# A hybrid decoder layer with a 16384-expert PEER block: order of the gathers in the second half's embedding, layout of the gate products, stored low parts, and which engines pad the value weights

## The chip, the cores and the metric

The kernel runs on one core of a Trainium2 chip. The core has TensorE (PE, matrix products, with its weight loads shown as PEld), VectorE (DVE), ScalarE (ACT), GpSimd (POOL) and SyncE (SP); SP and POOL issue all transfers here. The metric is the device time of one execution in microseconds. The result is compared as the median of several runs.

## The reference

One layer on 1024 tokens of width 1024, all in fp32. What matters here is what follows the mixer:

```python
mix = hybrid_mixer(x, ...)                       # z = x @ w_in, RG-LRU branch, GLA branch, m @ w_out
x   = layer_norm(DN_ALPHA * x + mix, ln1_g, ln1_b)
ple = sigmoid(x @ ple_gate_w) * (p @ ple_proj_w)
ffn = peer(x, ...)
x   = layer_norm(DN_ALPHA * x + ffn + ple, ln2_g, ln2_b)

def peer(x, w_q, sub_keys, u_tab, v_tab):
    q = (xt @ w_q).reshape(T, 8, 2, 64)
    s = einsum("thpc,hpkc->thpk", q, sub_keys)   # 8 heads, 2 halves, 128 keys
    top_s, top_i = top_k(s, 16)                  # per half
    ...                                          # 256 candidates -> best 16 per head
    gate = softmax(best_s)
    hid  = gelu(einsum("td,ted->te", xb, u_tab[expert_idx]))
    out  = einsum("te,ted->td", gate * hid, v_tab[expert_idx])
```

So each token picks 128 of 16384 experts. Each expert has a row of 1024 numbers in `peer_u` and one in `peer_v`.

## The kernel before

The 1024 tokens are eight tiles of 128, four to a half. The program does mixer, `post`, mixer, `post` for the two halves, and then `dense`.

**Two ways to compute PEER.** Four tiles (`GT` = 0, 1, 6, 7) gather. `gather_u` fetches, for each of 128 selections, one row of `peer_u` per token by an indirect transfer from POOL (a tile `ug` of 128 x 1024, 0.524 MB), and DVE multiplies it with x1 and sums (L849). `gather_v` fetches rows of `peer_v` by token (`vg`) and PE accumulates them in the PSUM tile `ffn` (L883): four rows make one step of 8 matmuls in the code. Their stationary operand `w32` is a zeroed tile into which a column of the weights is copied on a diagonal (L866, L869); eight such tiles serve a tile of tokens. `ug` and `vg` share one ring of 7 buffers, and of 11 in the dense stage. The other four tiles (`DT` = 4, 5, 2, 3) are computed densely against all experts: `dense_gates` builds for each token a 128 x 128 table of gate values as a matmul of one-hot operands into the PSUM tile `pg`, ACT copies it to `gst` (L990), and it goes to DRAM as `g_d`; `dense` then runs `hidden` and `value` over all 16384 experts.

**fp32 by three products.** Wide matmuls are made of three passes over operands split in a high and a low part (`split`, L259 and L260: ACT rounds, DVE subtracts). `weights` keeps the low part of a weight tile in DRAM in the first half and loads it in the second, so that DVE need not subtract again. The first 60 tiles in the order of the code are kept: the mixer's 56 and four of `w_out`. Not kept are four of `w_out`, eight of `peer_wq` (name `pq`), eight of `ple_gate_w` and four narrower ones of `ple_proj_w`.

**The order of the work.** The scheduler places instructions by priority on each engine; engines run their queues in order. The gathers are a generator beside the main program. `pump(t)` adds `t` times a rate (0.8, 0.6, 1.0, 1.2 in phases 0 to 3) to a credit and advances the generator while credit is left; each row costs 1.46, a routing step 0.7 to 2. `weave` goes round the three parts `us`, `routes`, `vs`, one step each. Phase 2 is the second half's `post` and runs with rate 1.0 at a priority 500 places later; phase 3 is `dense`, 10000 places earlier. Routing of a tile takes 16 selections of scores, the candidates, and the lookup of the keys, nearly all on DVE; tiles 0, 1, 4 and 5 are routed in line, tiles 2, 3, 6 and 7 by `routes`.

**The second half's `post`.** It multiplies by `w_out` (with two of the 32 gate steps after each quarter), normalises, scores the eight heads (a gate step after each), routes tiles 4 and 5, and then does the embedding: four quarters, each with four gate steps, a product with `ple_gate_w` (`plg`) and one with `ple_proj_w` (`plp`). `flow["scored"]` becomes 2 after the routing of tiles 4 and 5.

Of the kernel before, what the change touches and what calls it, by code (L numbers as in the profile page):

```python
# [8 lines left out]
F32 = mybir.dt.float32  # L9
# [4 lines left out]
AF = mybir.ActivationFunctionType  # L14
# [4 lines left out]
P = 128  # L19
# [5 lines left out]
NH = T // HT  # L25
TT = HT // P
# [4 lines left out]
KEYS = 128  # L31
# [22 lines left out]
KG = 4  # L54
RING = 6

LOW = 60

TG = 8

# [7 lines left out]
def kernel(ctx: ExitStack, tc: tile.TileContext, a: dict, out: bass.AP, tap=None):  # L68
    nc = tc.nc
# [8 lines left out]
    dram = ctx.enter_context(tc.tile_pool(name="dram", bufs=1, space=bass.MemoryType.DRAM))  # L78
# [141 lines left out]
    flow = {"it": None, "credit": 0.0, "rate": 0.0, "scored": 0, "phase": 0, "routing": False}  # L220
# [46 lines left out]
    def weights(src, name, shape):  # L267

        raw = early.pop(src.offset, None) if name == "zx" else None
        if raw is None:  # L270
            raw = wpool.tile(shape, F32, name=f"raw_{name}", tag="wraw")
            nc.sync.dma_start(raw, src)
        h = wpool.tile(shape, F32R, name=f"wh_{name}", tag="wh")
        l = wpool.tile(shape, F32R, name=f"wl_{name}", tag="wl")
        key = (src.tensor.name, src.offset)
        if low.get(key) is not None:
            nc.sync.dma_start(l.bitcast(F32), low[key])
            nc.scalar.activation(h, raw, AF.Copy)
        else:
            split(h, l, raw)  # L280
            if key not in low:
                n = len(low)
                low[key] = None
                if n < LOW:
                    low[key] = dram.tile(shape, F32, name=f"low{n}")
                    nc.sync.dma_start(low[key], l.bitcast(F32))
        return h, l

    low = {}
# [567 lines left out]
    def gather_v(ti, idx, idxT, gate, H):  # L857
        ffn = ps_f.tile([P, D], F32, name="ffn")
        nc.tensor.transpose(ffn[:, :P], H[0], ident)
        pw = small.tile([P, P], F32, name="pw")  # L860
        nc.scalar.activation(pw, ffn[:, :P], AF.Copy)
        N = 4
        for ph in range(32 // N):

            w32 = peer.tile([P, 4, N, 32], F32, name="w32", bufs=2)
            nc.vector.memset(w32, 0.0)  # L866
            for c in range(4):
                dst = w32[:, c].rearrange("p r e -> p (r e)")[:, ph * N:ph * N + (N - 1) * 33 + 1:33]
                nc.vector.tensor_copy(dst, pw[:, 32 * c + ph * N:32 * c + ph * N + N])  # L869
            for r in range(N):  # L870

                rows_v = []
                for c in range(4):
                    t = 32 * c + ph * N + r
                    vg = row("vg")
                    nc.gpsimd.indirect_dma_start(out=vg, out_offset=None, in_=a["peer_v"],  # L876
                                                 in_offset=bass.IndirectOffsetOnAxis(ap=idxT[:, t:t + 1], axis=0))
                    rows_v.append(vg)
                    if c < 3:
                        yield 1.46  # L880
                with ExitStack() as side:
                    for n, (e, c) in enumerate((e, c) for e in range(2) for c in (3, 0, 1, 2)):
                        mm = nc.tensor.matmul(ffn[32 * c:32 * c + 32, e * 512:(e + 1) * 512], w32[:, c, r],  # L883
                                              rows_v[c][:, e * 512:(e + 1) * 512], start=ph == 0 and r == 0,
                                              stop=ph == 32 // N - 1 and r == N - 1, skip_group_check=True)
                        if n == 0:

                            side.enter_context(tc.issue_after(mm.ins))
                            side.enter_context(tc.high_priority())
                yield 1.46  # L890
        ln2 = norm2()
        bt = row("bt")
        st = small.tile([P, 2, 6], F32, name="st2")
        nc.sync.dma_start(bt, base_d[ti])
        for e in range(2):
            es = slice(e * 512, (e + 1) * 512)
            nc.vector.scalar_tensor_tensor(bt[:, es], bt[:, es], 0.5, ffn[:, es], op0=ALU.mult, op1=ALU.add)
            nc.vector.bn_stats(st[:, e], bt[:, es])
        finish(ti, bt, st, ln2)

    def weave(*its):

        its = list(its)
        while its:
            stuck = True
            for it in list(its):
                x = next(it, None)
                if x is None:
                    its.remove(it)
                elif x >= 0:  # L910
                    yield x
                if x is None or x >= 0:
                    stuck = False
            if stuck:
                yield -1.0

    def gathers():

        H = {t: [] for t in GT}
        done = []  # L920

        def routes():
            while at[0] < ROUTE:
                yield -1.0
            for t in sorted((t for t in range(T // P) if t % TT >= DIRECT[t // TT]), key=lambda t: (t // TT, t in GT)):

                while t in GT and GT.index(t) > 2 and len(done) < GT.index(t) - 2:
                    yield -1.0
                while flow["scored"] <= t // TT:
                    yield -1.0  # L930
                flow["routing"] = True
                yield from route(t, t in DT, R)
                flow["routing"] = False

        at = [0]

        def us():
            for t in GT:
                while t not in R:
                    yield -1.0  # L940
                for x in gather_u(t, *R[t], H[t]):
                    at[0] += 1
                    yield x

        def vs():
            for t in GT:
                while not H[t]:
                    yield -1.0
                yield from gather_v(t, *R[t], H[t])
                done.append(t)  # L950

        yield from weave(us(), routes(), vs())

    def norm2():
# [7 lines left out]
    def dense_gates(n, g_b, gps, iota):  # L962
# [9 lines left out]
        for tb in range(P // 16):  # L972
            gs = g_b.tile([P, KEYS, 16], F32, name="gst", tag="g")
            for q in range(16 // TG):
# [5 lines left out]
                oj = g_b.tile(B3, F32, name="oj", bufs=2)  # L980
                nc.vector.tensor_tensor(oj, iota, Tb[:, 1, tt, None].to_broadcast(B3), op=ALU.is_equal)  # L981
                for r4 in range(TG // 4):
                    o = gps.tile([P, 4, KEYS], F32, name="pg", tag="g")
                    for r in range(4):
                        t = 4 * r4 + r
                        oi = g_b.tile([P, KEYS], F32, name="oi", bufs=6)
                        nc.scalar.activation(oi, one[:, t], AF.Copy, scale=T3[:, 2, t0 + t:t0 + t + 1])  # L987
                        nc.tensor.matmul(o[:, r], oj[:, t], oi, start=True, stop=True)  # L988
                    q4 = q * TG + 4 * r4
                    nc.scalar.activation(gs[:, :, q4:q4 + 4].rearrange("p i t -> p t i"), o, AF.Copy)  # L990
                    pump(0.9)
            nc.sync.dma_start(g_d[:, :, n * P // 16 + tb].rearrange("g j i t -> j g (i t)"),
                              gs.rearrange("p (g i) t -> p g (i t)", i=8))
# [194 lines left out]
```

## Time and profile before

| | |
|---|---|
| median of 3 runs | 3303.26 us (3296.75 to 3304.23) |
| the profiled execution | 3298.0 us, its span 3296.2 us |
| busy in the span | PE 3042.8, DVE 2375.3, ACT 1228.2, POOL 1160.8 us |
| HBM read, written | 854.76 MB, 81.79 MB |

The span runs from the first to the last instruction. Times within it are counted from its start. The second half's `post` begins near 1118 us, the gates end at 1613.6 us, and the dense stage follows, its first matmuls overlapping the last gates.

### The profile page before, as it was taken

How to read it: one execution, taken by the hardware profiler on the slowest of the kernel's cores; microseconds unless marked ns; L12 is line 12 of the kernel's file. 1: busy time of each engine (PE TensorE's matmuls, PEld its weight loads, DVE VectorE, ACT ScalarE, POOL GpSimd, SP SyncE). 2: the span in 40 equal slices, each digit the busy share in tenths (PEclk: the TensorE clock that was granted, in tenths of full speed). 3: DMA queues.
4: the chain of work that ended last, by engine and by line, in shares of the span. 5: the costliest groups of instructions: out<-in, count | busy, mean ns of one | idle time of the engine just before them, and what ended most of it. 6: DMA issues, size and time to landing. Idle time of an engine off the chain costs nothing.

```text
span 3296.2 us, 48127 instructions
## 1 busy us (share of the span) xinstructions
PE 3042.8 (92%) x17160; PEld 2320.6 (70%) x17160; DVE 2375.3 (72%) x5791; ACT 1228.2 (37%) x2130; POOL 1160.8 (35%) x1034
## 2 busy tenths in 40 slices
PE   8999989797999888658799999999999999999996
PEld 6788777676777676548577777777777777777663
DVE  7556557977888898978887866666666667666333
ACT  6433323263244464648623322222232232223221
POOL 0000000534421445540155444444434545443453
PEclk9999989898999998879899999999999999999997
DMA  5444444777776898976799899999899999988997
GB/s 174 143 172 148 135 160 142 277 293 284 295 263 244 326 312 302 349 252 216 246 376 352 321 338 327 340 338 344 314 340 326 355 335 326 338 328 327 346 322 277
DMA packets 364304, 939.74 MB, mean 285 GB/s; under 512 B 33920, under 2 KB 115968, under 8 KB 359968
## 3 DMA queue, kind: packets, MB, share of 16 engines
q0 software_dynamic: 147456, 536.94, 44.8%
q1 hardware_dynamic: 216608, 399.74, 34.8%
q8 instruction: 134, 2.20, 0.3%
q14 instruction: 106, 0.87, 0.1%
HBM read 854.76 MB, written 81.79 MB: 284 GB/s over the span
## 4 chain that ended last, share of the span: by engine, by line
PE 70%; DVE 14%; DMA 7%; ACT 4%; issue 3%; POOL 1%; SPq 0%; POOLq 0%; DVEq 0%; ACTq 0%
PE ph L263 7%; PE ph L265 7%; PE pv L265 7%; PE pv L263 7%; PE pv L264 7%; PE ph L264 7%; PE ffn L883 7%; DVE ug L849 3%; DMA ug<-in_peer_u_dram,idx 3%; DMA vg<-in_peer_v_dram,idxT 1%; DVE one L979 1%; DVE oj L981 1%; PE pgr L263 1%; PE pgr L264 1%; PE pgr L265 1%
## 5 line engine op out<-in xcount | busy, mean ns | idle before, releaser
L847 POOL DMA_INDIRECT ug<-in_peer_u_dram,idx x512 | 601.3, 1174 | 1345.1 <-DVE bs L776 612.3
L876 POOL DMA_INDIRECT vg<-in_peer_v_dram,idxT x512 | 558.2, 1090 | 756.7 <-DVE ug L849 324.3
L849 DVE SCALAR_TENSOR_TENSOR ug<-ug,x1g 128x1024 f32<-128x1024 f32 x512 | 619.8, 1219 | 47.0 <-DMA ug<-in_peer_u_dram,idx 42.9
L263 PE MATMUL ph<-x1hl,uh 128*128 128x512 f32 x1024 | 408.6, 399 | 0.9 <-DVE sc L737 0.9
L265 PE MATMUL ph<-x1hl,ul 128*128 128x512 f32 x1024 | 407.9, 398 | 0.0
L264 PE MATMUL ph<-x1hl,uh 128*128 128x512 f32 x1024 | 406.6, 397 | 0.0
L264 PE MATMUL pv<-vl,wdh 128*128 128x512 f32 x1024 | 400.5, 393 | 0.0
L263 PE MATMUL pv<-vh,wdh 128*128 128x512 f32 x1024 | 384.3, 393 | 15.9 <-ACT wdh L259 15.9
L265 PE MATMUL pv<-vh,wdl 128*128 128x512 f32 x1024 | 398.7, 393 | 0.0
L259 ACT ACTIVATE uh<-ur 128x512 fp32r<-128x512 f32 x256 | 160.2, 628 | 498.0 <-PE ph L264 489.2
L883 PE MATMUL ffn<-vg,w 128*32 128x512 f32 x2048 | 274.1, 628 | 51.1 <-DMA vg<-in_peer_v_dram,idxT 50.2
L259 ACT ACTIVATE vh<-vr 128x512 fp32r<-128x512 f32 x256 | 160.7, 629 | 356.9 <-PE pv L265 348.7
L260 DVE TENSOR_TENSOR ul<-ur,uh 128x512 fp32r<-128x512 f32 x256 | 175.7, 687 | 159.6 <-ACT uh L259 158.1
L260 DVE TENSOR_TENSOR vl<-vr,vh 128x512 fp32r<-128x512 f32 x256 | 176.3, 690 | 115.2 <-ACT vh L259 115.0
L1062 DVE SCALAR_TENSOR_TENSOR acc<-acc,pv 128x512 f32<-128x512 f32 x256 | 165.0, 681 | 108.8 <-PE pv L265 108.8
L263 PEld LDWEIGHTS pv<-vh,wdh 128*128 128x128 f32 x1024 | 192.8, 188 | 69.3 <-ACT wdh L259 16.1
L263 PEld LDWEIGHTS ph<-x1hl,uh 128*128 128x128 f32 x1024 | 192.4, 188 | 68.6 <-issue 22.6
L265 PEld LDWEIGHTS ph<-x1hl,ul 128*128 128x128 f32 x1024 | 192.4, 188 | 62.1 <-issue 16.8
L265 PEld LDWEIGHTS pv<-vh,wdl 128*128 128x128 f32 x1024 | 192.6, 188 | 58.7 <-issue 16.8
L264 PEld LDWEIGHTS ph<-x1hl,uh 128*128 128x128 f32 x1024 | 192.4, 188 | 55.7 <-issue 11.7
L264 PEld LDWEIGHTS pv<-vl,wdh 128*128 128x128 f32 x1024 | 192.9, 188 | 53.9 <-issue 10.1
L988 PE MATMUL pg<-oi,oj 128*128 128x128 f32 x1024 | 163.2, 301 | 35.9 <-ACT oi L987 25.4
(475 smaller groups left out, 6030.9 us busy)
## 6 DMA issues: line engine op xcount, KB each, us to landing
ur<-in_uT_dram SPq DMA_DIRECT2D x256, 256.0 KB, 6.3
vr<-in_peer_v_dram SPq DMA_DIRECT2D x256, 256.0 KB, 6.3
g_d<-gst SPq DMA_DIRECT2D x32, 1024.0 KB, 8.6
gt<-g_d SPq DMA_DIRECT2D x32, 1024.0 KB, 8.4
raw_zx<-in_w_z_dram SPq DMA_DIRECT2D x16, 512.0 KB, 4.9
raw_zv<-in_w_v_dram SPq DMA_DIRECT2D x16, 512.0 KB, 5.0
raw_zy<-in_w_z_dram SPq DMA_DIRECT2D x16, 512.0 KB, 6.4
raw_ga<-in_w_z_dram SPq DMA_DIRECT2D x16, 512.0 KB, 5.4
```

Of the source, the lines that this page charges most:

```text
L259: nc.scalar.activation(h, src, AF.Copy)
L260: nc.vector.tensor_tensor(l, src, h, op=ALU.subtract)
L263: nc.tensor.matmul(o, wh, xh, start=first, stop=False)
L264: nc.tensor.matmul(o, wh, xl, start=False, stop=False)
L265: nc.tensor.matmul(o, wl, xh, start=False, stop=last)
L847: nc.gpsimd.indirect_dma_start(out=ug, out_offset=None, in_=a["peer_u"], in_offset=bass.IndirectOffsetOnAxis(ap=idx[:, s:s + 1], axis=0))
L849: nc.vector.scalar_tensor_tensor(ug, ug, 1.0, x1, op0=ALU.mult, op1=ALU.mult, accum_out=hid[:, s:s + 1])
L876: nc.gpsimd.indirect_dma_start(out=vg, out_offset=None, in_=a["peer_v"], in_offset=bass.IndirectOffsetOnAxis(ap=idxT[:, t:t + 1], axis=0))
L883: mm = nc.tensor.matmul(ffn[32 * c:32 * c + 32, e * 512:(e + 1) * 512], w32[:, c, r], rows_v[c][:, e * 512:(e + 1) * 512], start=ph == 0 a ...
L979: nc.vector.tensor_tensor(one, iota, Tb[:, 0, tt, None].to_broadcast(B3), op=ALU.is_equal)
L988: nc.tensor.matmul(o[:, r], oj[:, t], oi, start=True, stop=True)
L1062: nc.vector.scalar_tensor_tensor(acc[c][:, es], acc[c][:, es], 0.5 if g == 0 else 1.0, o[c], op0=ALU.mult, op1=ALU.add)
```

## The change

It has four parts.

1. `embedding()` is true from the end of scoring in the second half to the end of phase 2. Then `weave` takes its parts in reverse order and stops after the first that advances, so that value rows come before routing and routing before u rows; `routes` also waits while it is true.
2. The matmul into `pg` writes key by key with the token innermost (a step of 16 bytes), and the copy to `gst` then reads PSUM in order and writes runs of four tokens.
3. Every low part except that of `peer_wq` is kept in DRAM: 16 more tiles.
4. The zeroing of `w32` goes from DVE to POOL, and the copy onto the diagonal from DVE to ACT.

```diff
--- before.py
+++ after.py
@@ -54,7 +54,7 @@
 KG = 4
 RING = 6
 
-LOW = 60
+OWN = ("pq",)
 
 TG = 8
 
@@ -278,12 +278,9 @@
             nc.scalar.activation(h, raw, AF.Copy)
         else:
             split(h, l, raw)
-            if key not in low:
-                n = len(low)
-                low[key] = None
-                if n < LOW:
-                    low[key] = dram.tile(shape, F32, name=f"low{n}")
-                    nc.sync.dma_start(low[key], l.bitcast(F32))
+            if name not in OWN and key not in low:
+                low[key] = dram.tile(shape, F32, name=f"low{len(low)}")
+                nc.sync.dma_start(low[key], l.bitcast(F32))
         return h, l
 
     low = {}
@@ -863,10 +860,10 @@
         for ph in range(32 // N):
 
             w32 = peer.tile([P, 4, N, 32], F32, name="w32", bufs=2)
-            nc.vector.memset(w32, 0.0)
+            nc.gpsimd.memset(w32, 0.0)
             for c in range(4):
                 dst = w32[:, c].rearrange("p r e -> p (r e)")[:, ph * N:ph * N + (N - 1) * 33 + 1:33]
-                nc.vector.tensor_copy(dst, pw[:, 32 * c + ph * N:32 * c + ph * N + N])
+                nc.scalar.activation(dst, pw[:, 32 * c + ph * N:32 * c + ph * N + N], AF.Copy)
             for r in range(N):
 
                 rows_v = []
@@ -898,12 +895,16 @@
             nc.vector.bn_stats(st[:, e], bt[:, es])
         finish(ti, bt, st, ln2)
 
+    def embedding():
+        return flow["phase"] == 2 and flow["scored"] == NH
+
     def weave(*its):
 
         its = list(its)
         while its:
             stuck = True
-            for it in list(its):
+            last = embedding()
+            for it in reversed(its) if last else list(its):
                 x = next(it, None)
                 if x is None:
                     its.remove(it)
@@ -911,6 +912,8 @@
                     yield x
                 if x is None or x >= 0:
                     stuck = False
+                    if last:
+                        break
             if stuck:
                 yield -1.0
 
@@ -926,7 +929,7 @@
 
                 while t in GT and GT.index(t) > 2 and len(done) < GT.index(t) - 2:
                     yield -1.0
-                while flow["scored"] <= t // TT:
+                while flow["scored"] <= t // TT or embedding():
                     yield -1.0
                 flow["routing"] = True
                 yield from route(t, t in DT, R)
@@ -980,14 +983,14 @@
                 oj = g_b.tile(B3, F32, name="oj", bufs=2)
                 nc.vector.tensor_tensor(oj, iota, Tb[:, 1, tt, None].to_broadcast(B3), op=ALU.is_equal)
                 for r4 in range(TG // 4):
-                    o = gps.tile([P, 4, KEYS], F32, name="pg", tag="g")
+                    o = gps.tile([P, KEYS, 4], F32, name="pg", tag="g")
                     for r in range(4):
                         t = 4 * r4 + r
                         oi = g_b.tile([P, KEYS], F32, name="oi", bufs=6)
                         nc.scalar.activation(oi, one[:, t], AF.Copy, scale=T3[:, 2, t0 + t:t0 + t + 1])
-                        nc.tensor.matmul(o[:, r], oj[:, t], oi, start=True, stop=True)
+                        nc.tensor.matmul(o[:, :, r], oj[:, t], oi, start=True, stop=True)
                     q4 = q * TG + 4 * r4
-                    nc.scalar.activation(gs[:, :, q4:q4 + 4].rearrange("p i t -> p t i"), o, AF.Copy)
+                    nc.scalar.activation(gs[:, :, q4:q4 + 4], o, AF.Copy)
                     pump(0.9)
             nc.sync.dma_start(g_d[:, :, n * P // 16 + tb].rearrange("g j i t -> j g (i t)"),
                               gs.rearrange("p (g i) t -> p g (i t)", i=8))
```

## Rows read from the trace of the kernel before

**Rows 1.** The page's first part, busy time by engine (share of the span, instructions)
```profile
PE 3042.8 (92%) x17160; PEld 2320.6 (70%) x17160; DVE 2375.3 (72%) x5791; ACT 1228.2 (37%) x2130; POOL 1160.8 (35%) x1034
```

**Rows 2.** Windows: length, PE, PEld, DVE, ACT, POOL busy; clock, DMA share, GB/s
```profile
545.00:635.00 90.00, 66.22 (x452) 62.23 (x451) 81.81 (x335) 19.69 (x34) 25.96 (x22) 0.84 0.57 201
...
1118.00:1380.00 262.00, 222.35 (x1541) 179.24 (x1534) 248.12 (x674) 173.90 (x389) 136.22 (x102) 0.92 0.95 326
1380.00:1620.00 240.00, 166.93 (x1086) 142.37 (x1085) 206.58 (x610) 156.66 (x369) 58.26 (x48) 0.84 0.75 240
...
1400.00:1460.00 60.00, 33.88 (x207) 23.19 (x211) 51.75 (x144) 21.66 (x54) 32.65 (x26) 0.73 0.74 252
1460.00:1550.00 90.00, 77.71 (x584) 74.32 (x577) 71.23 (x138) 74.44 (x181) 7.46 (x6) 0.92 0.66 203
1550.00:1620.00 70.00, 50.17 (x277) 42.93 (x276) 65.15 (x230) 58.18 (x132) 8.81 (x8) 0.90 0.81 248
1620.00:1830.00 210.00, 201.79 (x940) 146.79 (x941) 170.17 (x472) 59.59 (x100) 101.00 (x88) 0.97 0.92 344
1830.00:2430.00 600.00, 600.00 (x2804) 440.61 (x2803) 416.19 (x769) 173.81 (x293) 273.08 (x259) 1.00 0.91 334
```

**Rows 3.** Windows of value rows alone: PE, PEld, POOL busy, then clock, DMA
```profile
1460.00:1550.00 90.00, 1.54 (x16) 0.26 (x8) 3.83 (x3) 0.92 0.66 203
1550.00:1620.00 70.00, 0.00 (x0) 0.00 (x0) 4.95 (x5) 0.90 0.81 248
1620.00:1830.00 210.00, 24.96 (x192) 5.33 (x192) 47.62 (x44) 0.97 0.92 344
```

**Rows 4.** Chain that ended last, in order of time: start, duration, what
```profile
1656.75 1.85 PE ffn L883 x16
```

**Rows 5.** Waits, 1460 to 1550 and 1400 to 1460: total, times, longest
```profile
POOL vg L876 <- DVE ug L849: 80.6, 1, 80.6
...
PE ffn L883 <- DMA vg<-in_peer_v_dram,idxT: 25.0, 4, 12.2
```

**Rows 6.** Windows of u rows alone: DVE (two records a row), POOL busy, clock, DMA
```profile
1620.00:1830.00 210.00, 50.09 (x82) 53.38 (x44) 0.97 0.92 344
1830.00:2430.00 600.00, 157.59 (x257) 136.46 (x129) 1.00 0.91 334
```

**Rows 7.** Windows, DVE on one tile's score selections, then on its candidates
```profile
1620.00:1740.00 120.00, 20.76 (x128) 0.94 0.95 356
...
1550.00:1620.00 70.00, 7.65 (x65) 0.90 0.81 248
```

**Rows 8.** Groups by line: busy, mean ns of one, idle before and its releasers
```profile
L990 ACT ACTIVATE gst<-pg 128x512 f32<-128x512 f32 x128 | 133.3, 1054 | 14.0 <-DMA g_d<-gst 9.6 <-PE pg L988 4.2
L683 ACT ACTIVATE sc_st<-psc 128x512 f32<-128x512 f32 x32 | 17.5, 595 | 4.5 <-DVE list L739 4.2 <-PE psc L681 0.3
L988 PE MATMUL pg<-oi,oj 128*128 128x128 f32 x1024 | 163.2, 301 | 35.9 <-ACT oi L987 25.4 <-DVE oj L981 8.9 <-ACT gst L990 1.6
L263 PE MATMUL pv<-vh,wdh 128*128 128x512 f32 x1024 | 384.3, 393 | 15.9 <-ACT wdh L259 15.9
L260 DVE TENSOR_TENSOR wl_plg<-raw_plg,wh_plg 128x1024 fp32r<-128x1024 f32 x16 | 19.4, 1215 | 3.7 <-ACT wh_plg L259 3.6
L866 DVE MEMSET w<- 128x512 f32 x32 | 15.5, 485 | 26.1 <-PE ffn L883 25.2
L869 DVE COPY w<-pw 128x4 f32<-128x4 f32 x128 | 12.3, 194 | 0.3
L605 ACT ACTIVATE rs<-mv,eps_l 128x1 f32<-128x1 f32 x16 | 4.5, 292 | 58.1 <-DVE mv L603 43.2 <-DVE y L608 6.8 <-DVE acc L608 4.4
L214 POOL MEMSET qk<- 128x256 f32 x1 | 0.3, 302 | 0.0
```

## The prediction

> **What bounds the kernel now.** I read the totals first, then busy time by stage, then the rows' own instructions in those stages, the waits, and the groups by line. TensorE (PE) is busy for 3042.8 us [rows 1] of a span of 3296.2; the 253 us it lacks are all there is to win without removing matmuls. By stage [rows 2]: in the dense stage, 1830 to 2430, PE has no idle time at all, so there every matmul taken out shortens the kernel. Before it, PE idles for 39.7 us in 1118 to 1380 and for 73.1 in 1380 to 1620, while VectorE (DVE) is busy for 248 of 262 and for 207 of 240 us. So the second half's scoring and embedding are set by DVE and, once the gates run (1460 to 1620), by ScalarE (ACT) with 132.6 of 160; the dense stage is set by PE.
>
> Between the two lies a misfit. A step of four value rows gives `ffn` 16 recorded matmuls and takes PE 1.85 us [rows 3, 4]. From 1460 to 1620 one such step runs, and from 1620 to 1830, with PE full, twelve. The reason is in the waits: GpSimd's queue (POOL) stands for 80.6 us in one piece on a value gather whose buffer a u row holds, until DVE gets to that u row's product [rows 5].
>
> **Value rows first.** I walked the credits of `pump` through the code. Both kernels reach the second half's embedding with 52 or 53 u rows of tile 1 and as many value rows of tile 0 written. The embedding pumps 16 x 2.64 + 16 x 0.66 + 64 x 0.9 = 110 credits. Before, they bought rounds of a u row (1.46), a value row (1.46) and a routing step (about 1.1): 28 of each. After, they buy 75 value rows at 1.46, exactly the rest of tile 0, one u row and no routing. The trace agrees with the walk: 80 value rows at the embedding's end by the one, about 82 at 1620 by the other (46 left in the twelve steps that follow).
>
> So twelve steps leave the full stage: 12 x 1.85 = 22 us less PE work there [rows 3, 4]. They land where PE idles 58 us (1400 to 1620: 26.1 + 12.3 + 19.8) [rows 2]. Transfers allow it: that stretch moves 50.8 MB; 19 more rows of 0.524 MB and 5.2 MB of low parts make 66 MB, 300 GB/s, against 344 reached in 1620 to 1830. Term: -22.
>
> What leaves DVE in the embedding: 28 u rows at 1.22 us (50.09 us for 41 rows [rows 6]) = 34, tile 6's selects = 21 [rows 7], and 8 + 4 subtractions for low parts, 1.215 us each and half that for the narrower four [rows 8] = 12. DVE falls from 188 to 121 of 220 us. Tile 0's finish (its second norm, three loads and a store on SP's queue) follows its last value row into the embedding, into the room that DVE gains there.
>
> **Gates.** The eviction into `gst` writes single elements 64 bytes apart and takes 1054 ns; the score's eviction has the same size, reads PSUM too and writes runs, and takes 595 [rows 8]. The new one writes runs of four. Bounds: no gain, or 0.459 us x 128 = 59; I take nearly all, since the length of the runs is what differs; no row has runs of four. 29 us of that lie in the embedding, 29 before 1380.
>
> How much shorter does the embedding get? With the twelve steps PE needs 161.8 + 22 = 184 of the 220 us, so at most 36 us go, and none if other waits take the place. PE stood 25.0 us in four waits for value rows between 1400 and 1460 [rows 5], and these stay. I take a little under half of the 36. Term: -16 (0 to -36).
>
> From 1118 to 1380 ACT's 29 us lie under DVE, which is 95% busy. DVE loses 4 subtractions for `w_out` (4.9) and three or four blocks of `w32` at 0.485 + 4 x 0.194 = 1.26 us [rows 8], about 9 in all. Term: -6 (0 to -9).
>
> **What comes back.** The 28 u rows and 28 routing steps go to the start of the dense stage: 34 + 21 + about 8 for the candidates [rows 7], less 4 for three blocks of `w32`: 59 us more for DVE, which had 170 of 210 us there. Routing's four loads on SP's queue go with it, now among the u and v tiles' loads; a late one delays only routing, which tile 6's u rows need last. That makes 229: 19 us too many, pushed past 1830 where DVE has 184 of 600 us free. Against that the value rows of tile 1 can't start before u of tile 1 ends, so PE has only dense matmuls to do. The dense matmuls' own need of DVE is (416.2 - 157.6) / 600 = 0.43 us for each us of PE [rows 2, 6]. If the surplus comes wholly out of the splits, PE loses 19 / 0.43 = 44 us; if it is only late, nothing. I take a quarter. Term: +10 (0 to +44).
>
> **Low parts.** 16 more tiles are stored in the first half (four of `w_out`, eight of the gate, four narrower ones of the projection), 7.3 MB. Most of it falls into the first embedding, at 201 GB/s with PE idle 23.8 of 90 us [rows 2]. 5.2 MB more make 259 GB/s, under the 344 seen, so transfers hide it; SP's queue holds the loads behind each store until the subtraction is done. If that cover fails, 5.2 MB at 344 GB/s cost 15 us. Term: +3.
>
> **Padding.** 32 memsets leave DVE (485 ns each), and so do the 26.1 us for which DVE stood in front of them, nearly all for PE to give up `w32` [rows 8]. On POOL one costs between 0.30 us (half the size [rows 8]) and 0.60, against gathers of over 1 us; behind it wait gathers, and behind these DVE and PE. The 128 copies cost ACT between DVE's 0.194 and the 0.292 us of a one-element ACTIVATE [rows 8]: 25 to 37 us over the kernel, hidden in the dense stage where ACT is 29% busy [rows 2]. New is that a copy on ACT waits for POOL, and behind it stand ACT's splits, for which PE waits. Bounds 0 and 26 us; since POOL passes a free `w32` well ahead of the rows, I take +2.
>
> **Matmuls into every fourth word.** `pg` is now written with a step of 16 bytes. No row has such an output. The nearest row is again the eviction, which took 1054 / 595 = 1.77 times as long for single elements 64 bytes apart. Bounds: nothing, or 0.77 x 163 us, the group's time on PE, = 126 [rows 8]. I take nothing: PE takes 163.2 / 1024 = 0.159 us for 128 columns here and 384.3 / 1024 = 0.375 for 512 in the dense stage, so it gives PSUM its words more slowly here than PSUM is seen to take them. The Trainium skill (PSUM — Partial Sum Buffer, section "Specifications (TRN2)") speaks against that: it says that any non-contiguous access pattern slows matmuls significantly, and by it the second rival's 3346 would be the forecast.
>
> **Sum.** -22 - 16 - 6 + 10 + 3 + 2 = -29. The profiled execution took 3298.0 us, 1.8 over its span, and lies 5 under the median of 3303.3; set against the median this gives 3274.
>
> **Rivals.**
> *The dense stage starves.* Phase 3 puts gathers and routing 10000 places ahead of the splits, so DVE does them first. If DVE can be filled only to 90%, 189 of the 229 us fit, and 40 / 0.43 = 93 us of PE are lost in place of 10: -22 - 16 - 6 + 93 + 5 = +54, 3357. It decides from 19 us of splits not made up, as 44 us then meet the gain. For it: 81% busy there already. Against: PE was full at that 81%, and the surplus can be done late, with 184 us free behind it.
> *Strided PSUM.* At 1.77 times, PE has 63 us more in each half of the gate steps. The stretch 1400 to 1620 then needs 184 + 63 = 247 of 220 us, and 1118 to 1380 needs 222 + 63 = 285 of 262: -22 + 27 + 23 + 15 = +43, 3346. It decides once PE, not ACT, sets a gate step. For it speaks the eviction's row; against it that no matmul's row does. The rule quoted above would bring it about, and no run so far shows that.
> *Hidden anyway.* PE's queue stands for each late value row. Waits as in 1400 to 1460, some 6 us for a step, at six of the twelve moved steps take back 36 of the 38 us, and nothing measurable is left: 3303, give or take 9. For it: the 25.0 us. Against: then PE had little else to do.
> *All of it.* PE full through the embedding and no price after: -22 - 36 - 9 = -67, 3236. For it: three engines are relieved at once there.
>
> **Chances.** The forecast 0.46 (own range 3258 to 3293), starving 0.16, strided PSUM 0.08, hidden 0.15, all 0.15. A measurement of this kernel tells about 0.3%, 10 us. Faster: the forecast and "all", less a little at the edge, 0.60; same 0.16; slower 0.24. The range leaves out the worse half of the strided and starving cases and the better half of "all": 3236 to 3340.
>
> **What would show it.** Right: about 30 steps of `ffn` before the dense stage in place of 20; no 80 us wait of POOL on a u row there; `gst` near 600 ns; no u rows and no selects between 1460 and the dense stage; DVE over 90% in its first 200 us with PE still full. Wrong: PE idle time after the dense stage's start, matmuls into `pg` longer than 275 ns each, or waits of PE for value rows beyond 25 us.

## The result and the profile after

The changed kernel took 3332.48 us, the median of 4 runs (3327.47 to 3338.22); the kernel before took 3300.01 beside it (3295.29 to 3304.23). The ratio is 1.0106, with a 95% interval of 1.0090 to 1.0122: slower by about 1.1%, where 3274 and a gain were forecast. The profiled execution took 3327.47 us with a span of 3325.7.

The page of the changed kernel: busy time of PE, then PE's and DMA's busy tenths in 40 slices.

```profile
PE 3055.2 (92%) x17160; PEld 2323.9 (70%) x17160; DVE 2338.9 (70%) x5615; ACT 1198.5 (36%) x2258; POOL 1180.7 (36%) x1066
...
PE   8999988797999888888889999999999999999984
...
DMA  5444455877777999899995769999998999999898
```

PE is busy only 12 us longer than before [rows 1], and yet the span is 29.5 us longer. DMA has a hole in slices 22 to 24 (some 1745 to 1995 us), early in the dense stage, and PE's last slice is at 4. The same stages as in [rows 2], and PE's end (length, PE, PEld, DVE, ACT, POOL busy, clock, DMA share, GB/s):

```profile
1118.00:1380.00 262.00, 226.89 (x1568) 183.87 (x1566) 245.11 (x739) 157.85 (x407) 121.04 (x94) 0.93 0.94 325
1380.00:1620.00 240.00, 196.95 (x1333) 150.57 (x1334) 137.78 (x260) 139.57 (x385) 84.79 (x76) 0.91 0.95 328
1400.00:1460.00 60.00, 48.86 (x367) 39.54 (x366) 46.01 (x102) 42.90 (x125) 24.65 (x21) 0.91 0.87 292
1460.00:1550.00 90.00, 77.56 (x612) 64.98 (x610) 47.69 (x56) 65.99 (x192) 28.90 (x25) 0.94 1.02 338
1550.00:1620.00 70.00, 61.19 (x302) 41.59 (x302) 24.86 (x38) 27.96 (x62) 21.93 (x21) 0.92 0.94 342
1620.00:1830.00 210.00, 184.74 (x748) 146.76 (x747) 208.31 (x536) 63.19 (x104) 94.30 (x71) 0.93 0.79 290
...
3215.00:3307.00 92.00, 50.41 (x272) 9.06 (x260) 2.03 (x4) 2.76 (x13) 55.76 (x61) 0.69 0.98 372
```

And the value rows' matmuls alone, answering [rows 3] (PE, PEld, clock, DMA):

```profile
1400.00:1460.00 60.00, 10.05 (x64) 1.85 (x64) 0.91 0.87 292
1460.00:1550.00 90.00, 12.76 (x96) 2.59 (x96) 0.94 1.02 338
1550.00:1620.00 70.00, 11.15 (x80) 2.27 (x80) 0.92 0.94 342
1620.00:1830.00 210.00, 0.00 (x0) 0.00 (x0) 0.93 0.79 290
1830.00:1950.00 120.00, 0.00 (x0) 0.00 (x0) 1.00 0.60 213
3215.00:3307.00 92.00, 50.41 (x272) 9.06 (x260) 0.69 0.98 372
```

Up to 1620 the steps moved as planned: 15 `ffn` steps (240 records at 16 a step) in 1400 to 1620, 31 in all ahead of the first `pv` matmul where there were 20, PE busy 187.6 us in that stretch (184 forecast), DVE's load gone. At the dense start DVE is busy for 208.31 of 210 us, PE has 25.3 us of idle time in place of 8.2, and no value row is used from 1620 to 1950. At the end 17 `ffn` steps (272 records) run alone; before, there were three.

The gates' two edits, first the `pg` matmuls of the kernel before, then those of the changed one with their eviction (ns min/median/max, first and last start):

```profile
L988 PE MATMUL pg<-oi,oj x1024: 270/275/583, 1126.2 to 1612.1; 128*128 128x128 f32 x171
```

```profile
L991 PE MATMUL pg<-oi,oj x1024: 270/275/582, 1132.6 to 1565.6; 128*128 128x128 f32 x171
L993 ACT ACTIVATE gst<-pg x128: 572/584/612, 1134.0 to 1565.9; 128x512 f32<-128x512 f32 x128
```

The eviction fell from 1054 ns [rows 8] to 584, and the gates end 46.5 us earlier. The matmul into every fourth word takes what it took. On that point the measurement decides against the Trainium skill (PSUM — Partial Sum Buffer, section "Specifications (TRN2)"): a median of 275 ns either way, no slowdown for this non-contiguous write.

**Where the time went.** The gathers form a chain: u rows of a tile, its `hid`, its value rows beside the next tile's u rows, and so on through tiles 0, 1, 6 and 7. Its middle, in the kernel before (one tile's rows in 1760 to 2000, last two numbers the first and last start; `ffn<-ident,hid` is the transposition with which tile 1's value rows begin):

```profile
L859 PE MATMUL ffn<-ident,hid x1: 270/270/270, 1841.4 to 1841.4; 128*128 128x128 f32 x1
```

```profile
L832 PE MATMUL pidx<-ident,idf x1: 271/271/271, 1834.2 to 1834.2; 128*128 128x128 f32 x1
```

That `pidx` is tile 6's; tile 7's comes only at 2429.9 (2200 to 2600):

```profile
L832 PE MATMUL pidx<-ident,idf x1: 270/270/270, 2429.9 to 2429.9; 128*128 128x128 f32 x1
```

In the changed kernel both come ahead of tile 1's value rows; the last fence has the two longest waits of 1700 to 1960:

```profile
L850 ACT ACTIVATE hid<-hid x1: 312/312/312, 1772.6 to 1772.6; 128x128 f32<-128x128 f32 x1
...
L856 PE MATMUL ffn<-ident,hid x1: 271/271/271, 1946.0 to 1946.0; 128*128 128x128 f32 x1
```

```profile
L829 PE MATMUL pidx<-ident,idf x2: 271/272/272, 1835.3 to 1940.5; 128*128 128x128 f32 x2
```

```profile
POOL vg L873 <- PE ffn L880: 74.5, 1, 74.5
POOL ug L844 <- DVE idx L827: 71.9, 1, 71.9
```

POOL stands twice, and DMA's share falls with it. From 1759 to 1831 it stands for the indices of tile 6, whose routing the change has put into the dense start: tile 1's u rows are all fetched, and tile 6's can't be. From 1879 to 1954 it stands for an `ffn` step. Tile 1's `hid` was ready at 1772.6, 44 us earlier than before (1816.3), and was transposed only at 1946.0, 105 us later than before. `pidx` and `ffn` share one PSUM buffer. Before, tile 1's `ffn` took it ahead of tile 7's `pidx`; now tile 7's comes first, and DVE finishes that tile's routing only at 1940. Tile 7's routing isn't late, it is some 490 us early: `routes` holds it until tile 0's value rows are done, and these now end in the embedding.

From the start of tile 1's value rows to the last `ffn` matmul's start the chain takes 1435 us before (1841.4 to 3276.1), and 1360 now (1946.0 to 3305.6): 75 of the 105 us were made up, and the 30 that remain are the loss. The dense matmuls end 43 us earlier (last `pv` at 3214.1 in place of 3257.0) and gain nothing.

The transfers show the same loss. From 1950 to the last `ffn` matmul, before and then after (columns as in [rows 2]):

```profile
1950.00:3276.10 1326.10, 1315.56 (x6284) 940.09 (x6280) 817.20 (x1494) 363.86 (x609) 618.68 (x583) 0.99 0.92 334
```

```profile
1950.00:3305.60 1355.60, 1314.40 (x6260) 923.34 (x6259) 807.32 (x1398) 362.32 (x682) 667.34 (x640) 0.98 0.92 338
```

From 1620 to 1950 the changed kernel moves 26 MB less (262 GB/s in place of 341), and behind 1950 it moves 15 MB more (458 in place of 443), with DMA at 0.92 either way. Whether the order of the gathers or this share sets the pace behind 1950 is open.

The tail of the changed kernel (start, duration, and in brackets the idle time before it and its releaser):

```profile
3271.93 1.92 PE L880 MATMUL ffn<-vg,w 128*32 128x512 f32 x16 [1.79 <-DMA vg<-in_peer_v_dram,idxT]
3278.31 3.64 PE L880 MATMUL ffn<-vg,w 128*32 128x512 f32 x16 [4.46 <-DMA vg<-in_peer_v_dram,idxT]
...
3296.32 3.64 PE L880 MATMUL ffn<-vg,w 128*32 128x512 f32 x16 [6.98 <-DMA vg<-in_peer_v_dram,idxT]
3302.97 3.64 PE L880 MATMUL ffn<-vg,w 128*32 128x512 f32 x16 [3.01 <-DMA vg<-in_peer_v_dram,idxT]
```

PE waits for rows at nearly every step. The granted clock of this stretch is 0.69 on average; within single steps it is 1.00 or 0.50. A step takes 1.92 us at the upper level (2.4 GHz), near the 1.85 of the full stage [rows 4], and 3.64 at the lower (1.2 GHz).

### The profile page after: what moved, and what is told of

It reads as the page before. It is cut to its first block, busy times and chain, and to the rows that moved or that the text cites. A ratio compares the mean times of both kernels' runs of the same rounds, so it can differ in the third digit from the quotient of the medians.

```text
span 3325.7 us, 48251 instructions
## 1 busy us (share of the span) xinstructions
PE 3055.2 (92%) x17160; PEld 2323.9 (70%) x17160; DVE 2338.9 (70%) x5615; ACT 1198.5 (36%) x2258; POOL 1180.7 (36%) x1066
## 4 chain that ended last, share of the span: by engine, by line
PE 70%; DVE 13%; DMA 8%; issue 4%; ACT 4%; POOL 1%; SPq 0%; POOLq 0%; DVEq 0%; ACTq 0%
PE ffn L880 7%; PE ph L265 7%; PE ph L263 7%; PE ph L264 7%; PE pv L263 7%; PE pv L264 7%; PE pv L265 7%; DVE ug L846 5%; DMA vg<-in_peer_v_dram,idxT 3%; PE pg L991 2%; DMA g_d<-gst 2%; DMA ug<-in_peer_u_dram,idx 1%; PE pgr L263 1%; PE pgr L264 1%; PE pgr L265 1%
## 5 line engine op out<-in xcount | busy, mean ns | idle before, releaser
L880 PE MATMUL ffn<-vg,w 128*32 128x512 f32 x2048 | 286.1, 657 | 53.3 <-DMA vg<-in_peer_v_dram,idxT 53.2
L880 PEld LDWEIGHTS ffn<-vg,w 128*32 128x32 f32 x2048 | 58.2, 115 | 203.2 <-issue 137.7
```

## The experiments

They ran in groups, each group on one chip; the kernel before, run beside each, had medians from 3295.8 to 3319.4 us. So a ratio is taken against the kernel before on the same chip, and kernels are set against each other only within a group (those with the same number in brackets in the table). How far ratios of different groups can stand apart is seen on one kernel that ran in two: 0.9932 (0.9909 to 0.9954) and 0.9992 (0.9980 to 1.0004). Groups 3 and 5 bear the same chip number, so the chip alone doesn't explain it. The order on each engine is written by a planner, so each edit shifts instructions beyond its own; a few us of any difference can be that.

The table is read from the traces: start of tile 1's value rows; last `pv` and last `ffn` matmul (starts); PE and DVE busy in 1620 to 1830 (210 us).

| kernel | us (before beside it) | ratio | value rows 1 | last pv | last ffn | PE | DVE |
|---|---|---|---|---|---|---|---|
| before | | 1 | 1841.4 | 3257.0 | 3276.1 | 201.8 | 170.2 |
| after | 3332.5 (3300.0) | 1.0106 | 1946.0 | 3214.1 | 3305.6 | 184.7 | 208.3 |
| E1 (1) other parts alone | 3284.6 (3307.6) | 0.9929 | 1836.7 | 3237.6 | 3263.6 | 210.0 | 170.7 |
| E2 (1) value rows first alone | 3318.6 (3307.6) | 1.0034 | 1912.0 | 3268.6 | 3300.6 | 179.5 | 195.6 |
| E3 (1) u rows alone held | 3289.1 (3307.6) | 0.9941 | 1868.3 | 3264.5 | 3271.0 | 193.0 | 196.9 |
| E4 (1) tile 7's routing late | 3311.8 (3307.6) | 1.0011 | 1863.3 | 3263.2 | 3294.1 | 181.6 | 196.5 |
| E5 (2) both | 3278.5 (3295.8) | 0.9953 | 1800.8 | 3259.3 | 3249.3 | 192.1 | 201.4 |
| E9 (3) after, fewer matmuls | 3298.7 (3319.4) | | 2000.5 | 3031.2 | 3276.8 | 170.2 | 196.4 |
| E10 (3) before, fewer matmuls | 3225.6 (3319.4) | | 1848.7 | 3078.9 | 3203.5 | 180.2 | 181.0 |
| E11 (3) after, short products | 3312.6 (3319.4) | 0.9976 | 1911.5 | 3237.5 | 3291.9 | 191.3 | 171.1 |
| E12 (3) layout and padding | 3297.0 (3319.4) | 0.9932 | 1838.1 | 3253.0 | 3273.3 | 206.8 | 169.5 |
| E14 (4) as E5 | 3287.9 (3310.9) | 0.9936 | 1809.0 | 3267.7 | 3257.7 | 191.1 | 199.9 |
| E15 (4) E5, low parts as before | 3279.3 (3310.9) | 0.9911 | 1800.7 | 3260.4 | 3250.0 | 192.4 | 202.5 |
| E16 (4) E5, held to row 64 | 3276.9 (3310.9) | 0.9908 | 1798.6 | 3245.3 | 3247.0 | 209.3 | 185.7 |
| E17 (4) as E1 | 3286.6 (3310.9) | 0.9936 | 1837.6 | 3238.5 | 3264.4 | 210.0 | 170.8 |
| E18 (5) E16, low parts as before | 3271.0 (3296.4) | 0.9921 | 1811.4 | 3244.3 | 3249.3 | 209.7 | 187.8 |
| E19 (5) as E12 | 3293.5 (3296.4) | 0.9992 | 1833.5 | 3248.2 | 3269.2 | 208.5 | 168.8 |

### Which part costs, and through what: E1 to E4

E1 takes the reordering out of the changed kernel; E2 puts it alone (the hunks of `embedding`, `weave` and `routes`) into the kernel before.

```diff
     def embedding():
-        return flow["phase"] == 2 and flow["scored"] == NH
+        return False
```

> The changed kernel with the turn-taking of gathers as before (the other three parts of the change stay). Theory A: the end is set by the chain of gathers (u rows of tile 1, then value rows of tile 1 beside u rows of tile 6, and so on to tile 7's value rows), and the reordering is what delayed it, by about 75 us at u(7)'s end. Then tile 1's first ffn step is back near 1834 us, u(7) ends near 3000, and the time is 3275 to 3303, at or under the kernel before. Theory B, DVE's load at the start of the dense stage alone: same time as A here. Theory C, one of the other parts (padding rows by POOL and ScalarE, more low parts through DRAM, the strided PSUM tile) costs it: the time stays at 3320 to 3340.

> The kernel before with the reordering of the gathers alone. Theory A (chain of gathers): slower than before by 25 to 55 us, 3325 to 3355, with tile 7's indices transposed before tile 1's hid and the last value rows running alone after the dense matmuls. Theory C (another part costs the time): 3290 to 3310.

E1: 0.9929 (0.9904 to 0.9953), in the range of theories A and B; C, another part as the cause, falls. E2: 1.0034 (1.0017 to 1.0051), slower as A says, but by 11 us and not by 25 to 55; C's range holds the ratio nearly too, and only E1 rules it out. The parts don't add: -0.7% and +0.3% make +1.1% together. Theory A, as measured, says why. In E2 the last `ffn` starts at 3300.6, in the changed kernel at 3305.6: almost the same end of the chain. In E2 PE's dense work hid most of it (last `pv` 3268.6); the other parts bring that forward by 54 us (some 20 of them because 11 more `ffn` steps are left behind it), and the chain doesn't follow.

E3 holds back u rows alone; routing and value rows take turns. E4 leaves the embedding as changed and holds tile 7's routing until tile 1's value rows have begun.

```diff
-            for it in reversed(its) if last else list(its):
+            for it in its[1:] if last else list(its):
...
-                    if last:
-                        break
...
-                while flow["scored"] <= t // TT or embedding():
+                while flow["scored"] <= t // TT:
```

> The changed kernel, but in the embedding only u rows are held back; routing steps of tile 6 alternate with value rows, so about 7 ffn steps fewer leave the dense stage and 27 us of VectorE selects return to the embedding. In the order of TensorE's instructions tile 7's indices still come ahead of tile 1's hid. If the wait of tile 1's hid for tile 7's routing is the cost and VectorE's load makes it long (theory A with B as its size): 3290 to 3315. If u rows of tile 1 alone set the delay: 3320 to 3340.

```diff
-                while t in GT and GT.index(t) > 2 and len(done) < GT.index(t) - 2:
+                while t in GT and GT.index(t) > 2 and len(begun) < GT.index(t) - 1:
...
+                begun.append(t)
                 yield from gather_v(t, *R[t], H[t])
```

> The changed kernel, but tile 7's routing is held until tile 1's value rows have begun, so that tile 1's hid is transposed ahead of tile 7's indices, as before. Theory A with the shared PSUM slot as the cause: tile 1's first ffn step comes at 1800 to 1860 in place of 1952, and the time is 3285 to 3310. Theory B (VectorE's load at the dense start starves TensorE, slot or no slot): 3320 to 3340.

E4's middle of the chain, the two transpositions as shown above:

```profile
L856 PE MATMUL ffn<-ident,hid x1: 270/270/270, 1863.3 to 1863.3; 128*128 128x128 f32 x1
```

```profile
L829 PE MATMUL pidx<-ident,idf x1: 271/271/271, 1856.0 to 1856.0; 128*128 128x128 f32 x1
```

One `pidx` (tile 6's) in place of two, and the value rows begin 83 us earlier than in the changed kernel, 3 us over the range. The time lies between A's range and B's. How much this order is worth can't be told well: 12 us by the profiled spans, 21 by the medians, 31 by the ratios (1.0106 to 1.0011, 0.9998 to 1.0023), which are of different groups. Nor does E4 cure the slot wholly: tile 1's `hid`, ready at 1793.3, still waits 70 us, now for tile 6's `pidx`. In E4 the tail is 31 us long (3263.2 to 3294.1), and PE stands idle 28.4 of 210 us at the dense start. E3 (0.9941, 0.9920 to 0.9961; 1 us under its range) keeps tile 7's `pidx` ahead of tile 1's `ffn`, at 1863.0 in place of 1940.5, since tile 6's routing is mostly done in the embedding and its `pidx` comes at 1699.8; its tail is 7 us. So the wait at the slot is as long as the routing behind it is late.

POOL's longest waits from 1620 to 2020 tell the two losses apart (us; from the traces):

| kernel | for tile 6's indices | for an `ffn` step |
|---|---|---|
| before | none | 11.0 |
| after | 71.9 | 74.5 |
| E2 | 36.4 | 73.9 |
| E3 | none | 22.3 |
| E4 | 71.9 | 25.2 |
| E5 | none | 10.3 |
| E11 | 13.8 | 73.5 |

E3 takes away the first and cuts the second to 22 us, E4 cuts the second alone, E5 takes both down to what the kernel before had.

### The two cures together: E5

E3's and E4's edits in one kernel.

> The changed kernel with two edits: in the embedding only u rows wait (routing of tile 6 goes on), and tile 7's routing is held until tile 1's value rows have begun. Theory A (two separate losses: the chain of gathers, set by when tile 1's value rows begin, and VectorE full at the dense start): the chain ends before the last dense matmul, what is left is VectorE's load, TensorE idle 20 to 30 us between 1580 and 1850; 3278 to 3292, at or a little under the run in which u rows alone wait (0.994 of before). Theory B (VectorE's load is all of it): as that run or the run with late routing of tile 7, 3289 to 3312.

0.9953 (0.9935 to 0.9972), as theory A has it. The last `ffn` starts ahead of the last `pv`: the chain no longer ends the kernel. What is left stands at the dense start:

```profile
1620.00:1830.00 210.00, 192.12 (x822) 144.41 (x821) 201.36 (x505) 60.77 (x109) 119.51 (x97) 0.96 0.95 344
```

DVE 201 of 210 us, PE idle 17.9.

### The other parts one by one: E6 to E8, E12, E19

Each is put alone into the kernel before; the diffs are the hunks of the change.

> The kernel before with the gates' PSUM tile as key, token alone (TensorE writes with a step of four, ScalarE's eviction in runs of four). If this is what the three other parts give together (0.993 of before): 3275 to 3290, with the gates' last store 15 to 30 us earlier. If the strided write costs TensorE: 3310 or more. If the embedding's length is set by other things: 3295 to 3308.

> The kernel before with the low parts of all weights but the queries kept in DRAM, alone. From VectorE's relief in the second half's mixing and embedding: 3288 to 3303. If the added stores and loads set something: 3303 to 3320.

> The kernel before with w32's zeros written by GpSimd and its columns by ScalarE, alone. Theory C (padding in the queue of the gathers slows their chain): 3310 or more. Otherwise 3295 to 3308, no difference that can be told.

The gates' layout: 0.9973 (0.9961 to 0.9985), no cost from the strided write, but the last `pg` matmul starts at 1608.0, 4 us earlier and not 15 to 30; the gate steps alone take 476 us in place of 486 (433 in the changed kernel, 445 in E1, which has the low parts and the padding beside the layout). Low parts: 1.0031 (1.0019 to 1.0043), a cost of about 10 us. Padding: 1.0006 (0.9996 to 1.0015), nothing that can be told.

E12, and E19 in a later group, have layout and padding without the low parts:

> The kernel before with the gates' layout and the padding on GpSimd and ScalarE, without the low parts. If parts add up (0.9973 and 1.0006 alone): 0.997 to 0.999 of before. If the three parts together gain what none gains alone, and the low parts are the one that costs (1.0031 alone): 0.990 to 0.994.

> The kernel before with the gates' layout and the padding alone, once more beside the other: 0.992 to 0.997 of before. What the other has beyond it is what value rows ahead are worth when the chain of gathers keeps its order: 0.3 to 0.6%, or nothing if VectorE takes it back.

0.9932 and 0.9992 (over its range), medians of 3297.0 and 3293.5. The first would say that two parts gain what none gains alone, the second that they gain nothing; the kernel is the same, and what differs is how the kernel before stood beside it (3319.4 and 3296.4). How much of E1's 0.7% belongs to which part stays open.

### Does the chain set the end? E9, E10

One of the three products in `hidden` is left out, so that PE has some 233 us less to do in the dense stage; first in the changed kernel, then in the kernel before.

```diff
-                        mm3(o, uh[:, k], ul[:, k], X[0][:, 4 * n + k], X[1][:, 4 * n + k], n + k == 0, n * k == 3)
+                        nc.tensor.matmul(o, uh[:, k], X[0][:, 4 * n + k], start=n + k == 0, stop=False)
+                        nc.tensor.matmul(o, ul[:, k], X[0][:, 4 * n + k], start=False, stop=n * k == 3)
```

> The changed kernel, with one of the three products in each step of the dense stage's hidden layer left out (1024 matmuls of about 228 ns less, some 233 us of TensorE; the output is then less exact). Theory A, the chain of gathers sets the end: from the start of tile 1's value rows to the last ffn matmul stays near the 1361 us of the changed kernel, so the time falls by little, to 3260 to 3330, and TensorE idles instead. Rival, TensorE's work sets the end: 3090 to 3140.

> The kernel before with the same products left out. Theory A: the chain of gathers, which begins tile 1's value rows some 100 us earlier than in the changed kernel, sets the end here too once TensorE has less to do: 1841 + 1361 + 19 gives 3220, 3190 to 3250, some 75 to 105 us under the changed kernel with the same edit. Rival, TensorE's work: 3070 to 3110.

3298.74 and 3225.63 us, one run each, on one chip where the kernel before takes 3319.4. Start of tile 1's value rows, and PE's waits from 2400 to 3200 (total, times, longest), first E9, then E10:

```profile
L856 PE MATMUL ffn<-ident,hid x1: 272/272/272, 2000.5 to 2000.5; 128*128 128x128 f32 x1
```

```profile
PE ffn L880 <- DMA vg<-in_peer_v_dram,idxT: 89.0, 22, 14.5
```

```profile
L859 PE MATMUL ffn<-ident,hid x1: 271/271/271, 1848.7 to 1848.7; 128*128 128x128 f32 x1
```

```profile
PE ffn L883 <- DMA vg<-in_peer_v_dram,idxT: 53.2, 18, 5.6
```

The reader is to see that 233 us of matmuls bought the kernel before 94 (74 against the 3300.0 of the first comparison), and that the changed kernel, with the same matmuls, is 73 us behind it. Its chain began 152 us later and took 1276 us, E10's 1355; so it can be pressed by some 80 us more when PE has less to do, and the 1361 that theory A took for fixed is not. PE's work as the only bound (3090 to 3140, 3070 to 3110) falls. That the end is the gathers', theory A holds, but the start of tile 1's value rows doesn't set it by itself: over all kernels of the table the stretch from there to the last `ffn` takes 1276 to 1449 us, and E4, which begins it 83 us ahead of the changed kernel, ends it only 11.5 us ahead. A limit on the transfers is a rival that these two runs don't rule out: from 1950 to the last `ffn` DMA moves 333 to 338 GB/s at a share of 0.92 in every kernel with full matmuls, and 345 and 355 (0.93 and 0.96) in E9 and E10.

### Is it DVE's load? E11

The products of tile 1's u rows in the dense stage over 256 of 1024 columns.

```diff
+            n = 256 if flow["phase"] == 3 and ti == GT[1] else D
-            nc.vector.scalar_tensor_tensor(ug, ug, 1.0, x1, op0=ALU.mult, op1=ALU.mult, accum_out=hid[:, s:s + 1])
+            nc.vector.scalar_tensor_tensor(ug[:, :n], ug[:, :n], 1.0, x1[:, :n], op0=ALU.mult, op1=ALU.mult, accum_out=hid[:, s:s + 1])
```

> The changed kernel, with the products of tile 1's u rows that are made in the dense stage taken over 256 of 1024 columns (tile 1's expert weights are then wrong), which takes some 70 us of VectorE's work out of the dense start and leaves every transfer. If VectorE's load is what idles TensorE there and holds the routing: TensorE idle 1566 to 1850 falls from 32 us to under 12, tile 1's value rows begin 40 to 70 us earlier, and the time is 3250 to 3300. If transfers or the shared PSUM slot by itself hold the chain: 3315 to 3335.

Its dense start and what PE waited for longest there:

```profile
1620.00:1830.00 210.00, 191.26 (x792) 148.76 (x791) 171.10 (x621) 59.25 (x102) 99.11 (x92) 0.97 0.94 355
```

```profile
PE pv L264 <- DVE vl L260: 6.6, 3, 3.6
PE ph L265 <- DVE ul L260: 6.1, 3, 2.9
```

0.9976 (0.9959 to 0.9993), 3312.6 us: between the two ranges. Against the changed kernel that is 20 us by the medians and 14 by the profiled spans; the ratios say 43, but they are of different groups, and E12 shows how far this one stands off. DVE's load is part of it: the wait for tile 6's indices falls from 71.9 to 13.8 us, and tile 1's value rows begin 35 us earlier (1911.5), under the 40 expected. The wait at the slot stays (73.5), as tile 7's `pidx` still comes first. PE idles 27 us from 1566 to 1850 and not under 12; in 1620 to 1830 it is 18.7, with DVE no busier than in the kernel before, and PE waits for splits. So the sum of DVE's work is not all of it. That the splits stand behind bursts of selections and products in DVE's order would explain the rest, but was not tried by itself.

### What value rows ahead are worth with the chain in order: E14 to E18

Four kernels on one chip: E5 again, E5 with the 60 low parts of before (the hunk of `weights` undone), E5 with u rows held only until 64 value rows are out (the diff), and E1 again.

```diff
-            for it in its[1:] if last else list(its):
+            for it in its[1:] if last and flow.get("v", 0) < 64 else list(its):
...
-                yield from gather_v(t, *R[t], H[t])
+                for x in gather_v(t, *R[t], H[t]):
+                    flow["v"] = flow.get("v", 0) + 1
+                    yield x
```

> The kernel in which u rows alone are held and tile 7's routing is late, once more beside the others of this call. 0.993 to 0.997 of before. If value rows ahead are worth anything with the chain in order, it stands at least 0.2% under the three other parts alone; if VectorE's load at the dense start takes it all back, within 0.2% of them.

> The same kernel with the low parts of before (60 in DRAM). If the extra stores and loads cost 0.3% in the combination as alone: 0.990 to 0.993 of before. If VectorE's relief pays for them here: 0.994 to 0.998, at or over the kernel with them.

> As the first of this call, but u rows are held only until 64 of tile 0's value rows are out (22 ffn steps ahead of the dense stage's first value matmul in place of 27). By VectorE's load: TensorE idle between the gates' end and 1850 us falls under 15 us, and the 5 steps that come back cost 9 us, so within 0.2% of the first, either way. If the number of value rows ahead is what counts: 0.2 to 0.4% slower than the first.

> The three other parts alone, once more beside the others of this call: 0.991 to 0.998 of before.

E14 and E17 both come out at 0.9936. E14 has seven more steps ahead of the first `pv` (27 and 20) and no tail (E17's is 26 us), but its dense matmuls end 29 us later, with DVE at 200 of 210 us at their start: the two cancel. Without the added low parts E15 is at 0.9911 (0.9897 to 0.9925), 9 us under E14, about their price alone in E7. E16 is at 0.9908 (0.9891 to 0.9925), 11 us under E14, which neither reading had: 22 steps ahead of the first `pv` in place of 27, and PE full where DVE is at 186 of 210. (PE's idle time from the gates' end at 1558 to 1850 is 26 us, not under 15, but it lies before 1620.)

E18 puts E15's and E16's edits together, beside E19:

> Gates' layout, padding on GpSimd and ScalarE, u rows held until 64 of tile 0's value rows are out, tile 7's routing after tile 1's value rows have begun, low parts as before. If the two gains add: 0.987 to 0.990 of before. If they are one and the same relief of the same stage: 0.990 to 0.993.

```profile
1620.00:1830.00 210.00, 209.68 (x969) 152.84 (x968) 187.84 (x506) 65.30 (x119) 105.87 (x94) 1.00 0.92 338
```

0.9921 (0.9903 to 0.9939), median 3271.0: faster than the kernel before, like E16. Whether E15's and E16's gains add can't be told across groups; the ratio lies in the range of the reading that they are one relief. E19 beside it has 3293.5: value rows ahead, cut short at row 64 and with the chain in order, are worth 22.5 us there. Little of that is PE's work: E18 has only two steps more ahead of the first `pv` (22 and 20), and its last `pv` comes 4 us earlier. The other 16 us of the profiled spans' 20 are the tail (5 us in place of 21).

## Why the prediction was wrong

**The sum.** It added up PE's work and ended with it. Up to the last dense matmul its sign was right: that matmul comes 43 us earlier, where 29 were forecast. But 14 `ffn` steps that lay ahead of it before now lie behind it (17 in place of 3); at 1.85 us they make 26 of the 43, and 17 are left. The step that failed is the one that priced the delayed rows: DVE's surplus "if it is only late, nothing", and tile 1's value rows, which can't start before its u rows end, as a mere relief for PE. What is late there are the gathers, which set the end. It cost +72 us of tail (19.1 before, 91.5 now), and no term and no rival had it. The views that I read (totals, stages, waits) show PE full from 1830 to 2430 and don't show how soon the gathers come next (75 us were made up here). The starts of `hid`, `pidx` and `ffn`, and the three steps after the last `pv`, would have.

**Routing.** I wrote that a late load "delays only routing, which tile 6's u rows need last". Tile 6's u rows come right behind tile 1's, and POOL stood 71.9 us for their indices. And I missed tile 7's routing. With tile 0's value rows done in the embedding nothing holds it any more, so it comes into the dense start too, which the 229 us that I counted for DVE leave out, and takes the PSUM buffer of tile 1's `ffn`. POOL stood 74.5 us for that. E3, E4 and E5 show both by taking them away; what E4's order alone is worth is 12 to 31 us.

**Value rows first, -22.** 11 steps moved of the 12 forecast. What they save PE was measured nowhere by itself. That the best order stands 22.5 us ahead of the kernel without it (E18 against E19) is a chance agreement: two steps moved there, and most of the gain is the shorter tail.

**Embedding, -16 and -6.** Too small: the gate steps (first to last `pg`) take 433 us in place of 486, and they begin 6 us later. The value rows' waits that I took to stay did not stay: PE waits 3.4 us for them between 1400 and 1620, where it had 25.0 in 1400 to 1460 alone [rows 5].

**DVE's surplus, +10.** PE lost 17 us more than before in 1620 to 1830, inside 0 to 44. The starving rival was right in kind (DVE at 208 of 210) and far too dear at 93. *Hidden anyway* falls, since the moved steps did fit into PE's idle time; *all of it* had the gates nearer (36 and 9 against the 46.5 us by which they end earlier), without the prices behind it.

**Low parts, +3; padding, +2; strided PSUM, 0.** 10 us alone (E7), inside 0 to 15; 2 us (E8); nothing (275 ns, E6).

## What to carry to other kernels

When an engine is full in the last stage, removing work from it pays only until the next chain that runs through the stage ends: before summing, follow the transfers' chain from its last step back and read from the starts of its links how much delay it can take (here some 75 us). Work that is moved takes its buffers along: look which tag and slot the moved instruction shares, and who comes after it there. Work that ends earlier also lets loose what waited for its end, as tile 7's routing here. And when work moves into idle time, what it pushes out falls on the next stage: stop where that stage's engine is full; 22 steps ahead gave more here than 27.

## What the hardware showed unasked

- When PE, full until then, waits for each step's rows at the end, its granted clock goes from 1.00 (1830 to 2430) to 0.69, and at least seven of the last 17 `ffn` steps take 3.64 us each, near twice the 1.85 of the full stage. How much of the tail the slower steps cost beside the waits, no run shows.
- Runs of four words were enough for the eviction: 584 ns, against 1054 for single words and 595 for whole runs [rows 8].
- GpSimd's memset of 128x512 takes 541 ns, inside the 0.30 to 0.60 us taken for it.
